# Scaling the experts' tokens by 1/rms once, at the turn, and modulating a whole gather on ScalarE

## The chip, the cores and the metric

The kernel runs on one core of one Trainium2 chip. The metric is the device time of one execution in microseconds; three runs of the kernel before gave 1472.24 to 1476.46, with a median of 1474.25. The core's engines each work through their own queue in order: TensorE (PE in the profile) multiplies and turns matrices, VectorE (DVE) and ScalarE (ACT) work on elements, SyncE (SP) starts the transfers from memory. They wait for each other by semaphores.

## The reference, cut to what matters

A two-layer backbone over 256 tokens of width 1024. The change concerns only the second half of its second layer, a mixture of eight experts, of which each token goes to its best two. What goes into it is the stream `h`, brought to unit rms, scaled and shifted per channel:

```python
def rmsnorm(x, g):
    xf = x.astype(jnp.float32)
    y = xf * lax.rsqrt(jnp.mean(xf * xf, axis=-1, keepdims=True) + EPS)
    return (y * g.astype(jnp.float32)).astype(x.dtype)

def modulate(x, g, shift, scale):
    return rmsnorm(x, g) * (1 + scale) + shift

def swiglu(h, wg, wu, wd):
    return (jax.nn.silu(h @ wg) * (h @ wu)) @ wd

def moe_swiglu(h, router_w, wg, wu, wd):
    logits = (h @ router_w).astype(jnp.float32)
    top_v, top_i = lax.top_k(logits, TOP_K)
    gates = jax.nn.softmax(top_v, axis=-1)
    ...
    out = jnp.zeros_like(h)
    for e in range(N_EXPERTS):
        out = out + dense_gate[..., e:e + 1] * swiglu(h, wg[e], wu[e], wd[e])
    return out
```

Each expert has `wg` and `wu` of 1024 x 3584 and `wd` of 3584 x 1024, in fp32. The result is added to the stream, which is the output.

## The kernel before

**Products.** fp32 values go through PE as pairs of a rounded value ("hi") and the rest ("lo"). A heavy expert (more than 64 tokens) takes three products per pair (lines 142 to 144, in `mm3`), a light one two (lines 1078 and 1079); which arm runs is decided on PE by a branch on the expert's count.

**The turn of the tokens.** The stream lies transposed in `hT` (channels on partitions). Its sums of squares give `rstd`, two columns of 1/rms for the two times 128 tokens (`mo_v` in the trace). Sixteen PE transposes turn the tokens into four banks `mo{t}{b}` of PSUM, and ACT copies each bank (128 x 512) into `h`, in which tokens lie on partitions (L1001). `h` isn't scaled by `rstd`. Beside it run the router: `lg`, the ranks, `posm` (each token's place in each expert) and `gates()` with an exponent on ACT (L1031), for which ACT loads a table of functions.

**An expert's gather.** `Expert.positions()` makes one-hot matrices from `posm` on DVE: `oh`, `ohd` (each place twice, for light experts) and `ohs`, which is `oh` with `rstd` in the place of the ones (L1098). `gather(b)` picks the expert's tokens, for the channels' lower (b = 0) and upper half (b = 1): eight PE products `h` x `ohs` into one bank (`m_pg`, L1109), then the modulation `t32 = pg * a + b` in four pieces of 128 x 128 (`m_t`): for b = 0 on DVE (L1118), for b = 1 on ACT (L1116). `split_pairs` makes the hi (ACT, L217) and lo (DVE, L218) of `xg`, the input of the gate and up products. Both halves use one bank in turn, since that pool has one buffer; expert 0 takes two banks of another pool.

**The weights.** Each expert is worked in seven chunks of 512 columns; a chunk has three groups of two tiles of 1 MB: gate, up, and the down tiles of the chunk before. The class `Weights` brings in the 336 tiles: `load` starts a transfer on SP's queue into a raw buffer (`mw`), `split` casts it to hi on ACT (`mh`, L948) and takes hi from it to lo on DVE (`ml`, L949). `group()` runs the products of a group, splits the tiles of the groups ahead between them and then runs closures put off until there (`late`). Positions and both halves of the gather for the next expert are put off in this way, too: they stand behind the fifth chunk (`ci == NCH - 3`) of each expert, positions there, the halves behind one group each (`after(0)`, `after(1)`).

**The end of an expert.** The down products end in two banks; `gated` and `scatter` multiply them back to the tokens' places and add them on DVE: `acc = ps * gate + was` (L1184). For expert 0 `was` is `h` itself (the stream), so that the stream is added; for the others it is `acc`.

**What sets the order.** The Tile scheduler puts the instructions of each engine in an order from dependences and its own costs. By hand only a little is fixed: `behind["A"]` holds the first casts of weights behind the last copy of `h` (`copied`) on ACT, `behind["V"]` the first subtractions behind expert 0's `xg` (`ex.made`) on DVE.

Of the kernel before, what the change touches and what calls it, by code (L numbers as in the profile page):

```python
# [13 lines left out]
AF = mybir.ActivationFunctionType  # L14
ALU = mybir.AluOpType
# [3 lines left out]
P = 128  # L19
D = 1024  # L20
KT = D // P
S = 256
NT = S // P
# [51 lines left out]
def hybrid_kernel(  # L75
# [6 lines left out]
    V, A, T = nc.vector, nc.scalar, nc.tensor  # L82
# [13 lines left out]
    def slot(i, name, dt=F32):  # L96
        return ap_.tile([P, 2056 if i == 7 else 2048], dt, tag=f"s{i}", name=name)

    def x2k(name, dt=F32):
        return xp.tile([P, 512], dt, tag="x2k", name=name)  # L100

    def bank(name, pool=None):
        pool = pool or psa
        return pool.tile([P, 512], F32, tag="bank", name=name)
# [36 lines left out]
    def mm3(o, lh, ll, rh, rl, start, stop):  # L141
        T.matmul(o, lh, rh, start=start, stop=False)  # L142
        T.matmul(o, lh, rl, start=False, stop=False)  # L143
        T.matmul(o, ll, rh, start=False, stop=stop)  # L144
# [213 lines left out]
    def flush():  # L358
        while waiting:
            waiting.pop(0)()  # L360
# [76 lines left out]
    def mod_tiles(s_hi, s_lo, name):  # L437
        return tuple(slot(i, f"{name}_{x}", F32R)[:, :KT * S].rearrange("p (k t) -> p k t", k=KT) for i, x in ((s_hi, "hi"), (s_lo, "lo")))
# [10 lines left out]
    class Rows:  # L449
# [6 lines left out]
        def one(self, i, k, wh, wl):  # L456
            hi, lo, t, _ = self.specs[i]
            mm3(self.pss[i], hi[:, k, t * P:(t + 1) * P], lo[:, k, t * P:(t + 1) * P], wh, wl, start=(k == 0), stop=(k == KT - 1))
# [200 lines left out]
    y = mod_tiles(2, 3, "y")  # L659
# [294 lines left out]
    m_m = Mod(1, 3, 0, R_FFN + KT, "a_m")  # L954
# [30 lines left out]
    gate = kp.tile([P, NT, NE], F32, name="gate")  # L985
# [6 lines left out]
        next_ada()  # L992
    del behind["T"]
    rstd = st.rstd()
    h = slot(2, "h")[:, :NT * D].rearrange("p (t d) -> p t d", t=NT)
    for t in range(NT):
        for b in range(2):
            pt = bank(f"mo{t}{b}", psc)
            for i in range(4):
                T.transpose(pt[:, i * P:(i + 1) * P], hT[:, 4 * b + i, t * P:(t + 1) * P], ident)  # L1000
            copied = A.copy(h[:, t, b * 512:(b + 1) * 512], pt)  # L1001
    behind["A"] = copied.ins
    lg = kp.tile([P, NT, NE], F32, name="lg")
    for t in range(NT):
# [39 lines left out]
        return nc.values_load(flag[0:1, 0:1], min_val=0, max_val=1)  # L1044

    at = slot(3, "moe_aT", F32R)
    acc = slot(4, "moe_acc")[:, :NT * D].rearrange("p (t d) -> p t d", t=NT)
    iota = cst[:, C_IOTA:C_IOTA + P]

    def pick(w, e, *at):  # L1050
# [9 lines left out]
    def split_pairs(v, src):  # L1060
        return split_to(v[:, :, :, 0], v[:, :, :, 1], src.rearrange("p (k s) -> p k s", s=P))
# [24 lines left out]
    class Expert:  # L1086
# [5 lines left out]

        def positions(self):
            oh2 = x2k(self.n + "_oh")
            self.oh, self.ohs = oh2[:, :S], oh2[:, S:]
            self.ohd = x2k(self.n + "_ohd")[:, :S]
            for t in range(NT):
                V.tensor_scalar(self.ohs[:, t * P:(t + 1) * P], iota, one(self.pos, t, self.e), rstd[t], op0=ALU.is_equal, op1=ALU.mult)  # L1098
            for t in range(NT):
                for o, at_ in ((self.oh, iota), (self.ohd, twice)):  # L1100
                    V.tensor_scalar(o[:, t * P:(t + 1) * P], at_, one(self.pos, t, self.e), None, op0=ALU.is_equal)

        def gather(self, b, pool=None):
            n = self.n
            pg = bank(f"{n}_pg{b}", pool or psd)
            for i in range(4):
                k = 4 * b + i
                for t in range(NT):
                    T.matmul(pg[:, i * P:(i + 1) * P], h[:, t, k * P:(k + 1) * P], self.ohs[:, t * P:(t + 1) * P],  # L1109
                             start=(t == 0), stop=(t == NT - 1))  # L1110
            t32 = x2k(f"{n}_t{b}")
            for i in range(4):
                k = 4 * b + i
                o = slice(i * P, (i + 1) * P)
                if b:
                    A.activation(t32[:, o], pg[:, o], AF.Identity, bias=m_m.b(k), scale=m_m.a[:, k:k + 1])  # L1116
                else:
                    V.tensor_scalar(t32[:, o], pg[:, o], m_m.a[:, k:k + 1], m_m.b(k), op0=ALU.mult, op1=ALU.add)  # L1118
            self.made = split_pairs(self.xg[:, 4 * b:4 * b + 4], t32)

        def places(self, light):
# [19 lines left out]
        def turn(self, pts, gu, light):  # L1141
            for pt, src in zip(pts, gu):
                for i in range(4):
                    o = pt[:, i * P:(i + 1) * P]
                    if light:
                        T.matmul(o, src[:, i * P:(i + 1) * P], fold, start=True, stop=True)
                    else:
                        T.transpose(o, src[:, i * P:(i + 1) * P], ident)
# [26 lines left out]
            split_to(*y, src)  # L1175
            return y

        def scatter(self, t, i, y, first=False, pool=None):

            ps = bank(f"{self.n}_sc{t}{i}", pool or psd)  # L1180
            for o in range(2):
                T.matmul(ps, self.ohT[:, t * P:(t + 1) * P], y[o], start=(o == 0), stop=(o == 1))
            av, was = (a[:, t, i * 512:(i + 1) * 512] for a in (acc, h if first else acc))
            V.scalar_tensor_tensor(av, ps, one(gate, t, self.e), was, op0=ALU.mult, op1=ALU.add)  # L1184

    def store(t, i):
        nc.sync.dma_start(out[0, t * P:(t + 1) * P, i * 512:(i + 1) * 512], acc[:, t, i * 512:(i + 1) * 512])
# [20 lines left out]
    def after(n, f):  # L1208
        todo_after.setdefault(step + n, []).append(f)
# [19 lines left out]
    def turned(x, ci, gu):  # L1229
        pts = [bank(f"{x.n}_{ci}_t{m}", psb) for m in range(2)]  # L1230
        return pts, (lambda arm: x.turn(pts, gu, arm)), (lambda: x.act(ci, pts))
# [3 lines left out]
    for e in range(NE):  # L1235
        light = lights[e]
        for ci in range(NCH):
            gu = []
            _, turn, acted = turned(ex, ci - 1, prev[2]) if ci else nothing
            if ci:  # L1240
                behind.clear()
            o = bank(f"{ex.n}_{ci}_0")
            places = ci == 0
            if places:
                ex.po = bank(ex.n + "_ohp", psb)

            def gates_up(parts, arm, o=o):
                turn(arm)
                if places:
                    ex.places(arm)  # L1250
                ex.up(o, parts, arm)

            def gates_then(o=o, ex=ex, ci=ci, gu=gu, acted=acted, places=places):
                if places:
                    ex.placed()
                acted()
                gu.append(ex.copied(o, f"{ex.n}_{ci}_g"))

            group(light, gates_up, gates_then)
            u = bank(f"{ex.n}_{ci}_1")  # L1260
            group(light, lambda parts, arm: ex.up(u, parts, arm), lambda u=u, x=ex, ci=ci, gu=gu: gu.append(x.copied(u, f"{x.n}_{ci}_u")))
            if (e, ci) == (0, 1):
                over = gates()
                flush()
            if prev is not None:
                px, pi, _ = prev
                if pi == 0:
                    px.y = [bank(f"{px.n}_y{i}", psc) for i in range(2)]
                if ci == NCH - 1:
                    _, turn, acted = turned(ex, ci, gu)  # L1270
                else:
                    turn, acted = nothing[1:]

                def downs(parts, arm):
                    px.down(pi, parts, arm)
                    turn(arm)

                def downs_then(acted=acted, px=px, pi=pi):
                    acted()
                    if pi == NCH - 1:  # L1280
                        ys = [px.gated(i) for i in range(2)]
                        for i in range(2):
                            for t in range(NT):
                                after(1 + 2 * i + t, lambda x=px, t=t, i=i: x.scatter(t, i, ys[i], first=x.e == 0))

                group(lights[px.e], downs, downs_then)
            if ci == NCH - 3 and e + 1 < NE:
                nxt = Expert(e + 1, posm, (e + 1) % 2, f"m{e + 1}")
                nxt.positions()
                for b in range(2):  # L1290
                    after(b, lambda b=b, x=nxt: x.gather(b))
            prev = (ex, ci, gu)
        last = ex
        if e + 1 < NE:
            ex = nxt
            lights[e + 1] = nc.values_load(few[0:1, e + 1:e + 2], engines=(mybir.EngineType.PE,), min_val=0, max_val=1)
    for i in range(2):
        group(lights[-1], lambda parts, arm: last.down_half(i, parts, arm))
        y = last.gated(i)
# [5 lines left out]
    with tc.If(over > 0):  # L1305
        pos2 = sp.tile([P, NT, NE], F32, tag="pos2", name="pos2")
        V.tensor_scalar(pos2, posm, -float(P), None, op0=ALU.add)
        with tc.For_i(0, NE) as ev:
# [9 lines left out]
            for ci in range(NCH):  # L1318
                gu = []
                for m in range(2):  # L1320
                    o = bank(f"v_{ci}_{m}")
# [6 lines left out]
            for i in range(2):  # L1328
                y = ex.gated(i)
# [57 lines left out]
```

## Time and profile before

| | |
|---|---|
| median of three runs | 1474.25 us (1472.24 to 1476.46) |
| profiled execution | 1478.5 us, span in the trace 1476.7 us |
| TensorE, busy | 1390.9 us (94%) |
| TensorE, weight loads | 1151.7 us (78%) |
| VectorE, busy | 1226.8 us (83%) |
| ScalarE, busy | 974.0 us (66%) |
| the chain that ended last, by engine | PE 59%, DVE 20%, issue 9%, ACT 8%, DMA 5% |
| read from memory | 470.64 MB |
| the 336 subtractions of L949 | 757.1 us busy, 2286 ns each |
| the 336 casts of L948 | 631.2 us busy, 1910 ns each |

Busy time is the time in which an engine had an instruction running, as a share of the span; overlapping instructions of one engine are not counted twice. The chain is followed back from the last instruction to what released it each time; "issue" is time in which the engine waited for nothing that the profile shows. The experts run from about 507 us to the end, one behind the other, in stretches of 90 to 131 us, so that shares over the span mix two layers and eight stretches; stretches are looked at apart below.

### The profile page before, as it was taken

The page shows a single profiled execution, that of the slowest core. Times are in us where ns is not written, and L with a number is a line of the kernel's source. Part 1 is how long each engine was busy: PE and PEld are TensorE (multiplying, and loading weights), DVE is VectorE, ACT ScalarE, POOL GpSimd, SP SyncE. Part 2 cuts the span into 40 slices and gives each one's busy share as a digit, 9 for nine tenths or more (in the row PEclk, how much of TensorE's full clock was granted, in tenths as well). Part 3 has the DMA queues.
Part 4 walks back from the last instruction along what each step waited for, and adds up shares of the span by engine and source line. Part 5 has one row for each costly group of instructions (what it writes and reads, how often), then busy time and mean ns, then how long its engine had stood idle before and what let it go on. Part 6 is the DMA issues. An engine that isn't in the chain of part 4 may idle for free.

```text
span 1476.7 us, 19854 instructions
## 1 busy us (share of the span) xinstructions
PE 1390.9 (94%) x7746; PEld 1151.7 (78%) x7746; DVE 1226.8 (83%) x1256; ACT 974.0 (66%) x891; POOL 1.9 (0%) x7
## 2 busy tenths in 40 slices
PE   6999999999999999999989989999999999899897
PEld 4667789999979888877767767777888888677675
DVE  4687588776666698899999998998888879899897
ACT  3444354433354576788887887886777768788785
POOL 0000000000000000000000000000000000000000
PEclk9999999999999999999999999999999999999999
DMA  9554488776654698899998998998978988899894
GB/s 367 226 219 166 155 335 323 286 274 251 245 224 176 240 402 330 326 340 395 403 398 343 408 398 334 416 385 338 365 294 331 365 343 349 331 421 386 336 413 189
DMA packets 66784, 473.53 MB, mean 321 GB/s; under 512 B 7376, under 2 KB 7760, under 8 KB 9696
## 3 DMA queue, kind: packets, MB, share of 16 engines
q1 hardware_dynamic: 66464, 471.16, 82.0%
q8 instruction: 93, 1.52, 0.4%
q0 software_dynamic: 192, 0.56, 0.2%
q14 instruction: 35, 0.29, 0.1%
HBM read 470.64 MB, written 1.05 MB: 319 GB/s over the span
## 4 chain that ended last, share of the span: by engine, by line
PE 59%; DVE 20%; issue 9%; ACT 8%; DMA 5%; DVEq 0%; SPq 0%; ACTq 0%
DVE ml L949 13%; ACT mh L948 5%; PE m L142 5%; PE m L144 5%; PE m L143 5%; PE fg_ps L164 4%; PE fd L164 4%; PE fu_ps L164 4%; PE m_y L144 2%; PE m_y L142 2%; PE m_y L143 2%; PE so_ps L164 2%; PE ada L259 2%; PE su_ps L164 2%; DMA mw<-in_moe_w_gate_dram 1%
## 5 line engine op out<-in xcount | busy, mean ns | idle before, releaser
L949 DVE TENSOR_TENSOR ml<-mw,mh 128x2048 fp32r<-128x2048 f32 x336 | 757.1, 2286 | 47.9 <-ACT mh L948 44.9
L948 ACT CAST mh<-mw 128x2048 fp32r<-128x2048 f32 x336 | 631.2, 1910 | 12.4 <-PE so_ps L164 4.1
L1079 PE MATMUL m<-ml,m_xg 128*128 128x512 f32 x560 | 223.3, 399 | 5.7 <-DVE ml L949 5.7
L1078 PE MATMUL m<-mh,m_xg 128*128 128x512 f32 x560 | 224.1, 400 | 0.0
L1078 PE MATMUL m_y<-mh,moe_aT 128*128 128x512 f32 x280 | 118.2, 422 | 25.3 <-DVE moe_aT L218 21.4
L142 PE MATMUL m<-mh,m_xg 128*128 128x512 f32 x336 | 134.5, 401 | 0.6 <-ACT m_xg L217 0.6
L1079 PE MATMUL m_y<-ml,moe_aT 128*128 128x512 f32 x280 | 121.3, 433 | 13.8 <-DVE ml L949 11.9
L1079 PEld LDWEIGHTS m<-ml,m_xg 128*128 128x128 f32 x560 | 105.2, 188 | 37.0 <-DVE ml L949 14.6
L144 PE MATMUL m<-mh,m_xg 128*128 128x512 f32 x336 | 132.9, 396 | 0.0
L143 PE MATMUL m<-ml,m_xg 128*128 128x512 f32 x336 | 132.7, 395 | 0.0
L1078 PEld LDWEIGHTS m<-mh,m_xg 128*128 128x128 f32 x560 | 105.3, 188 | 22.6
L1079 PEld LDWEIGHTS m_y<-ml,moe_aT 128*128 128x128 f32 x280 | 56.4, 201 | 45.3 <-DVE ml L949 34.3
L1078 PEld LDWEIGHTS m_y<-mh,moe_aT 128*128 128x128 f32 x280 | 56.7, 203 | 41.3 <-ACT mh L948 19.3
L217 ACT CAST moe_aT<-m_sg 128x512 fp32r<-128x512 f32 x56 | 37.4, 669 | 72.5 <-DVE m_sg L1153 72.5
L142 PEld LDWEIGHTS m<-mh,m_xg 128*128 128x128 f32 x336 | 65.6, 195 | 13.3 <-ACT m_xg L217 1.5
L144 PEld LDWEIGHTS m<-mh,m_xg 128*128 128x128 f32 x336 | 65.5, 195 | 12.5
L143 PEld LDWEIGHTS m<-ml,m_xg 128*128 128x128 f32 x336 | 65.7, 196 | 11.9
L1152 ACT ACTIVATE m_sg<-m_t 128x512 f32<-128x512 f32 x56 | 33.6, 599 | 53.5 <-PE m L142 26.7
L144 PE MATMUL m_y<-mh,moe_aT 128*128 128x512 f32 x168 | 66.4, 396 | 0.7 <-DVE moe_aT L218 0.7
L143 PE MATMUL m_y<-ml,moe_aT 128*128 128x512 f32 x168 | 66.4, 395 | 0.0
L142 PE MATMUL m_y<-mh,moe_aT 128*128 128x512 f32 x168 | 66.2, 396 | 0.0
L164 PE MATMUL fd<-a,fd_hi 128*128 128x256 f32 x352 | 63.0, 281 | 0.0
(410 smaller groups left out, 2663.8 us busy)
## 6 DMA issues: line engine op xcount, KB each, us to landing
mw<-in_moe_w_gate_dram SPq DMA_DIRECT2D x112, 1024.0 KB, 7.1
mw<-in_moe_w_up_dram SPq DMA_DIRECT2D x112, 1024.0 KB, 7.1
mw<-in_moe_w_down_dram SPq DMA_DIRECT2D x110, 1024.0 KB, 6.8
ada<-in_ada_w_dram SPq DMA_DIRECT2D x40, 1024.0 KB, 4.9
fg_w<-in_ffn_w_gate_dram SPq DMA_DIRECT2D x11, 1024.0 KB, 5.2
fu_w<-in_ffn_w_up_dram SPq DMA_DIRECT2D x11, 1024.0 KB, 5.4
fd<-in_ffn_w_down_dram SPq DMA_DIRECT2D x11, 1024.0 KB, 5.0
adap<-in_ada_pairs_dram SPq DMA_DIRECT2D x8, 1024.0 KB, 9.6
```

The source lines that it names most:

```text
L142: T.matmul(o, lh, rh, start=start, stop=False)
L143: T.matmul(o, lh, rl, start=False, stop=False)
L144: T.matmul(o, ll, rh, start=False, stop=stop)
L164: self.newest = m = T.matmul(o, lhsT, rhs, start=self.first is None, stop=stop, skip_group_check=True)
L217: A.copy(hi, src)
L259: queued(T.matmul(pa[32 * j:32 * j + 32, :r.shape[2]], stat[:, 4 * half + j, :], r[:, j, :], start=(first and half == 0), stop=(last and h ...
L948: queued(A.copy(hi, r), "A")
L949: queued(V.tensor_tensor(lo, r, hi.bitcast(F32), op=ALU.subtract), "V")
L1078: T.matmul(o, x, wh, start=start, stop=False)
L1079: T.matmul(o, x, wl, start=False, stop=stop)
L1152: A.activation(sg, pts[0], AF.Silu)
```

## The change

At the turn, each bank is now read by ACT twice: copied into `acc` (unscaled, the stream that the experts are added to), and copied times `rstd` into `h`. For this `acc` is made here, together with `h`; the two lie in slots of their own. `ohs` goes, and `oh` takes its place in the gather's products, since `h` already has the factor; `ohd` moves into the buffer that `ohs` had. The modulation is done by ACT in both halves of a gather. `scatter` always adds to `acc`.

```diff
@@ the turn of the tokens
-    h = slot(2, "h")[:, :NT * D].rearrange("p (t d) -> p t d", t=NT)
+    h, acc = (slot(i, n)[:, :NT * D].rearrange("p (t d) -> p t d", t=NT) for i, n in ((2, "h"), (4, "moe_acc")))
...
-            copied = A.copy(h[:, t, b * 512:(b + 1) * 512], pt)
+            at_ = slice(b * 512, (b + 1) * 512)
+            A.copy(acc[:, t, at_], pt)
+            copied = A.activation(h[:, t, at_], pt, AF.Copy, scale=rstd[t])
@@ Expert.positions
-            self.oh, self.ohs = oh2[:, :S], oh2[:, S:]
-            self.ohd = x2k(self.n + "_ohd")[:, :S]
-            for t in range(NT):
-                V.tensor_scalar(self.ohs[:, t * P:(t + 1) * P], iota, one(self.pos, t, self.e), rstd[t], op0=ALU.is_equal, op1=ALU.mult)
+            self.oh, self.ohd = oh2[:, :S], oh2[:, S:]
@@ Expert.gather
-                    T.matmul(pg[:, i * P:(i + 1) * P], h[:, t, k * P:(k + 1) * P], self.ohs[:, t * P:(t + 1) * P],
+                    T.matmul(pg[:, i * P:(i + 1) * P], h[:, t, k * P:(k + 1) * P], self.oh[:, t * P:(t + 1) * P],
...
-                if b:
-                    A.activation(t32[:, o], pg[:, o], AF.Identity, bias=m_m.b(k), scale=m_m.a[:, k:k + 1])
-                else:
-                    V.tensor_scalar(t32[:, o], pg[:, o], m_m.a[:, k:k + 1], m_m.b(k), op0=ALU.mult, op1=ALU.add)
+                A.activation(t32[:, o], pg[:, o], AF.Identity, bias=m_m.b(k), scale=m_m.a[:, k:k + 1])
@@ Expert.scatter
-            av, was = (a[:, t, i * 512:(i + 1) * 512] for a in (acc, h if first else acc))
-            V.scalar_tensor_tensor(av, ps, one(gate, t, self.e), was, op0=ALU.mult, op1=ALU.add)
+            av = acc[:, t, i * 512:(i + 1) * 512]
+            V.scalar_tensor_tensor(av, ps, one(gate, t, self.e), av, op0=ALU.mult, op1=ALU.add)
```

The scheduler's order changes with it. On ACT at the turn of the tokens, before; `mo_48..` are the banks with the turned tokens, `ex` the exponents of the gates, `ada_11_rw` a row of the modulation of this layer, `mh` the first casts of weights:

```order
L1001 COPY h<-mo_4855 128x512
L1031 ACT_TABLE_LOAD
L1031 ACTIVATE ex_5127<-lg,mx_5124 128x8
L264 COPY ada_11_rw<-ada_10_4796 128x512
L1001 COPY h<-mo_4861 128x512
L948 CAST mh_4946<-mw_4932 128x2048
```

The same place in the changed kernel, with `mo_v` the 1/rms:

```order
L1002 COPY moe_acc<-mo_4851 128x512
L1003 ACTIVATE h<-mo_4844,mo_v 128x512
L1003 ACTIVATE h<-mo_4851,mo_v 128x512
L1033 ACT_TABLE_LOAD
L1033 ACTIVATE ex_5128<-lg,mx_5125 128x8
L264 COPY ada_11_rw<-ada_10_4796 128x512
L1002 COPY moe_acc<-mo_4858 128x512
L1003 ACTIVATE h<-mo_4858,mo_v 128x512
L1002 COPY moe_acc<-mo_4865 128x512
L1003 ACTIVATE h<-mo_4865,mo_v 128x512
L948 CAST mh_4947<-mw_4933 128x2048
```

Two scaled copies now stand ahead of the table load, and four passes instead of one between the row of the modulation and the first cast.

On ACT in expert 1, where its sixth chunk meets the gather for expert 2, before (`m_5_g` and `m_5_u` are that chunk's gate and up results, copied; branches are the end of a light expert's arm):

```order
L1138 COPY m_5_g<-m_5_0_6867 128x512
L948 CAST mh_6938<-mw_6745 128x2048
L948 CAST mh_6967<-mw_6758 128x2048
L1194 UNCONDITIONAL_BRANCH
L1138 COPY m_5_u<-m_5_1_6937 128x512
L217 CAST m_xg<-m_t_6960 128x512
L948 CAST mh_7014<-mw_6805 128x2048
L1116 ACTIVATE m_t_7031<-m_pg_7022,modT,a_m 128x128 x4
L948 CAST mh_7038<-mw_6813 128x2048
L1194 UNCONDITIONAL_BRANCH
L217 CAST m_xg<-m_t_7031 128x512
```

The same place in the changed kernel:

```order
L1133 COPY m_5_g<-m_5_0_6862 128x512
L1113 ACTIVATE m_t_6955<-m_pg_6946,modT,a_m 128x128 x3
L948 CAST mh_6933<-mw_6743 128x2048
L1113 ACTIVATE m_t_6955<-m_pg_6946,modT,a_m 128x128
L217 CAST m_xg<-m_t_6955 128x512
L948 CAST mh_6962<-mw_6756 128x2048
L1189 UNCONDITIONAL_BRANCH
L1133 COPY m_5_u<-m_5_1_6932 128x512
L1113 ACTIVATE m_t_7026<-m_pg_7017,modT,a_m 128x128
L948 CAST mh_7009<-mw_6803 128x2048
L1113 ACTIVATE m_t_7026<-m_pg_7017,modT,a_m 128x128 x3
L217 CAST m_xg<-m_t_7026 128x512
```

Three of the first half's `m_t` stand ahead of the first cast and one behind it; of the second half's, one stands ahead of the third cast and three behind it. The first half's `m_xg` has moved ahead of the second cast.

On PE, the second half of that gather stands in one piece before, behind the down products:

```order
L144 MATMUL m_y_6220<-mh_6938,moe_aT 128x512
L1194 UNCONDITIONAL_BRANCH
L1109 MATMUL m_pg_7022<-m_oh,h 128x128 x8
L1194 COMPARE_AND_BRANCH
L1146 MATMUL m_5_t_7085<-fold,m_5_g 128x128 x4
```

In the changed kernel, from the end of the up products to the end of the down products:

```order
L144 MATMUL m_5_1_6932<-mh_6863,m_xg 128x512
L1189 UNCONDITIONAL_BRANCH
L1107 MATMUL m_pg_7017<-m_oh,h 128x128 x5
L1189 COMPARE_AND_BRANCH
...
L144 MATMUL m_y_6218<-mh_6933,moe_aT 128x512
L1189 UNCONDITIONAL_BRANCH
L1107 MATMUL m_pg_7017<-m_oh,h 128x128 x3
L1189 COMPARE_AND_BRANCH
L1141 MATMUL m_5_t_7080<-fold,m_5_g 128x128 x4
```

Five of the eight products have moved ahead of the down products, three stay behind them.

## Rows read from the trace of the kernel before

**Rows 1.** Windows: stretch, length, PE, PEld, DVE, ACT, POOL busy, PEclk, DMA share, GB/s.

```profile
510.00:600.00 90.00, 90.00 (x418) 75.89 (x417) 76.66 (x52) 66.57 (x51) 0.00 (x0) 1.00 0.91 353
627.00:742.00 115.00, 105.69 (x516) 83.47 (x515) 110.90 (x78) 96.41 (x81) 0.00 (x0) 1.00 0.97 380
742.00:858.00 116.00, 104.51 (x492) 81.54 (x491) 110.22 (x77) 95.11 (x80) 0.00 (x0) 0.97 0.96 382
974.00:1103.00 129.00, 127.45 (x592) 107.09 (x590) 110.93 (x77) 94.81 (x79) 0.00 (x0) 1.00 0.90 341
```

**Rows 2.** Groups, 732 to 848: count | busy us, mean ns | idle before.

```profile
L1118 DVE TENSOR_SCALAR m_t<-m_pg,a_m,modT 128x128 f32<-128x128 f32 x4 | 1.4, 404 | 0.0
L1098 DVE TENSOR_SCALAR m_oh<-cst,posm,mo_v 128x128 f32<-128x128 f32 x2 | 0.7, 342 | 0.0
```

**Rows 3.** Timeline of DVE in expert 1: start, us, instruction, count [idle before <-releaser].

```profile
705.97 0.34 DVE L1098 TENSOR_SCALAR m_oh<-cst,posm,mo_v 128x128 f32<-128x128 f32 x1
706.23 0.28 DVE L1101 TENSOR_SCALAR m_oh<-cst,posm 128x128 f32<-128x128 f32 x1
...
717.02 0.40 DVE L1118 TENSOR_SCALAR m_t<-m_pg,a_m,modT 128x128 f32<-128x128 f32 x1
717.35 2.28 DVE L949 TENSOR_TENSOR ml<-mw,mh 128x2048 fp32r<-128x2048 f32 x1
...
726.73 2.29 DVE L949 TENSOR_TENSOR ml<-mw,mh 128x2048 fp32r<-128x2048 f32 x1 [1.13 <-ACT mh L948]
...
732.94 6.69 DVE L949 TENSOR_TENSOR ml<-mw,mh 128x2048 fp32r<-128x2048 f32 x3
```

**Rows 4.** Timeline of ACT in the same stretch, around the gather.

```profile
714.34 0.67 ACT L217 CAST moe_aT<-m_sg 128x512 fp32r<-128x512 f32 x1 [1.15 <-DVE m_sg L1153]
...
715.38 3.72 ACT L948 CAST mh<-mw 128x2048 fp32r<-128x2048 f32 x2
...
720.62 0.67 ACT L217 CAST m_xg<-m_t 128x512 fp32r<-128x512 f32 x1 [1.05 <-DVE m_t L1118]
721.18 1.89 ACT L948 CAST mh<-mw 128x2048 fp32r<-128x2048 f32 x1
723.40 1.50 ACT L1116 ACTIVATE m_t<-m_pg,modT,a_m 128x128 f32<-128x128 f32 x4 [0.33 <-PE m_pg L1109]
724.78 1.91 ACT L948 CAST mh<-mw 128x2048 fp32r<-128x2048 f32 x1
...
733.09 3.72 ACT L948 CAST mh<-mw 128x2048 fp32r<-128x2048 f32 x2
```

**Rows 5.** Timeline of PE in the same stretch: first down product, then the gather's products.

```profile
717.27 0.45 PE L1078 MATMUL m_y<-mh,moe_aT 128*128 128x512 f32 x1
...
721.41 1.95 PE L1109 MATMUL m_pg<-m_oh,h 128*128 128x128 f32 x16
```

**Rows 6.** Timelines of ACT, DVE and PE at the turn, to the first expert product.

```profile
494.49 1.07 ACT L1001 COPY h<-mo 128x512 f32<-128x512 f32 x2 [0.16 <-PE mo L1000]
495.58 1.28 ACT L1031 ACT_TABLE_LOAD   x1
...
499.87 0.58 ACT L1001 COPY h<-mo 128x512 f32<-128x512 f32 x1
500.35 3.70 ACT L948 CAST mh<-mw 128x2048 fp32r<-128x2048 f32 x2
...
505.94 0.65 ACT L217 CAST m_xg<-m_t 128x512 fp32r<-128x512 f32 x1
...
497.01 0.28 DVE L210 SCALAR_TENSOR_TENSOR mo_v<-mo_a,mo_y 128x1 f32<-128x1 f32 x2
...
501.20 3.73 PE L1109 MATMUL m_pg<-m_oh,h 128*128 128x128 f32 x32
...
506.65 0.51 PE L142 MATMUL m<-mh,m_xg 128*128 128x512 f32 x1 [0.64 <-ACT m_xg L217]
```

**Rows 7.** Timelines of PE and DVE, and a window, at the start of expert 2.

```profile
769.64 0.76 PE L1078 MATMUL m_y<-mh,moe_aT 128*128 128x512 f32 x1 [4.59 <-DVE moe_aT L218]
...
776.78 0.75 DVE L1184 SCALAR_TENSOR_TENSOR moe_acc<-m_sc,gate,moe_acc 128x512 f32<-128x512 f32 x1 [4.43 <-PE m_sc L1182]
...
769.00:777.00 8.00, 7.10 (x18) 5.30 (x18) 3.57 (x4) 6.05 (x5) 0.00 (x0) 0.59 0.92 353
```

More of the change, by code (lines that the diff above doesn't have):

```diff
@@ L1046, in hybrid_kernel @@
     at = slot(3, "moe_aT", F32R)
-    acc = slot(4, "moe_acc")[:, :NT * D].rearrange("p (t d) -> p t d", t=NT)
     iota = cst[:, C_IOTA:C_IOTA + P]
@@ L1176, in gated, with scatter @@
             return y
-        def scatter(self, t, i, y, first=False, pool=None):
+        def scatter(self, t, i, y, pool=None):
             ps = bank(f"{self.n}_sc{t}{i}", pool or psd)
@@ L1283, in downs_then @@
                             for t in range(NT):
-                                after(1 + 2 * i + t, lambda x=px, t=t, i=i: x.scatter(t, i, ys[i], first=x.e == 0))
+                                after(1 + 2 * i + t, lambda x=px, t=t, i=i: x.scatter(t, i, ys[i]))
                 group(lights[px.e], downs, downs_then)
```

## Prediction

> **What bounds the kernel now.** I read the page first, then the stretches by window, then single queues. Before 480 us nothing that the diff touches runs. From 510 on the kernel turns through eight experts with two regimes. In the first one TensorE (PE) is busy all the time (510 to 600: 90.00 of 90 us); 974 to 1103, and 1103 to 1234 like it, are also PE's (127.45 of 129). In 742 to 858 it is VectorE (DVE) that has 110.22 of 116 us and PE 104.51; 627 to 742 is like it [rows 1], and so are 858 to 974 and 1234 to 1349. So there are three experts at PE's pace (0, 4, 5: all three products per pair) and five at DVE's (1, 2, 3, 6, 7: two products). A gather of the next expert stands in experts 0 to 6; four of these seven (1, 2, 3, 6) are at DVE's pace. Time taken from DVE can count only there.
>
> Within such an expert a tile of weights goes DMA, ACT cast (mh), DVE subtraction (ml), PE. ACT has 95.11 of 116 us [rows 1], so it looks free; but it is one queue in order, and the timeline around a gather shows how little room its casts have. DVE waits 1.13 us for a cast at 726.73 [rows 3], because ACT had first waited 1.05 us for DVE's modulation (720.62), then 0.33 for PE, then run four m_t [rows 4]. That is the place to look at: the change takes work from DVE and puts it in front of those casts.
>
> **The change, part by part.**
>
> *DVE's saving in a gather.* Two m_oh with rstd and four m_t leave: 0.7 and 1.4 us of busy time [rows 2]. An instruction begins a little before the end of the one ahead, so what counts is the distance of starts: 705.97 to 706.23 for m_oh (0.26), 717.02 to 717.35 for m_t (0.33) [rows 3]. 2 x 0.26 + 4 x 0.33 = 1.8 us per gather; 4 x 1.8 = 7.3 us in the experts at DVE's pace. This is the most that can be won there. In experts 0, 4 and 5 PE's work covers it.
>
> *ACT's addition in a gather.* Four more m_t: the four of now take 723.40 to 724.78, 0.345 each [rows 4], so 1.4 us. It is not spread: three of the four stand ahead of the cast that starts at 715.38 and the fourth, with m_xg, behind it; of the second half one stands ahead of the cast of 721.18, three ahead of that of 724.78.
>
> *Whether the 1.8 us arrive.* I walk expert 1's gather with the new order and the durations of [rows 3, 4]. DVE reaches the chunk's splits 0.5 us earlier (m_oh). The scheduler then puts m_sg one split earlier, which makes ACT's m_sg, that waits for PE's turn, go ahead of a cast; that cast starts later by about as much, so DVE's gain of 0.5 is used up. ACT's moe_aT no longer waits until 714.34 but runs at 711.7, m_5_g at 714.0, when PE has its input, then three m_t: the cast of 715.38 starts at 715.5, its DVE partner at 717.5 instead of 717.35, with DVE idle 0.95 before it. The last m_t of the first half and m_xg end at 718.3; nothing waits for DVE's modulation now, so the 1.05 us of idle at 720.62 go. The cast of 721.18 starts at 720.85. Then three m_t wait for the last three products of the gather. These stand on PE behind the same down products as now and come at 723.4, when the sixteen m_pg of now end (721.41 + 1.95) [rows 5]: PE does five of the eight products before the down products, but needs the same work by then. So m_t runs at 723.5 to 724.5, m_xg to 725.2, and the cast of 724.78 starts at 725.1, 0.3 later; DVE idles 1.1 us before its partner, about as at 726.73 today. The next casts are 0.7 and 1.6 us early, but ACT's moe_aT waits for DVE's m_sg, which now stands behind one more split, at 731.4, and behind moe_aT and m_g stands the cast of 733.09, which by this starts at 733.2. Its DVE partner is the second of the three at 732.94: 735.1 then and now. From there the order is that of before until the next gather. So DVE's 1.8 us turn into 2 us of waits for ACT, and the gain per expert is 0 (between -1.8, if ACT keeps its lead, and +1.4, if all that ACT gets is late). I take -0.1 each, -0.4 in four.
>
> *The wait that is new on PE.* Both halves of a gather share one bank; the second half's five products, now ahead of the down products, wait for ACT's fourth m_t (717.8), and queued behind them are the down products. PE comes there at 717.3 [rows 5] and the second tile of the down products is not split before 719.6 (717.35 + 2.28), so 0.5 us of wait cost nothing in experts at DVE's pace. In those at PE's pace 24 up products stand on PE between the two halves of the gather, 6.2 us (16 down products take 717.27 to 721.41, 0.26 each [rows 5]); the four m_t and a cast among them take 1.4 + 1.9: covered, unless that cast is late by more than 2 us.
>
> *The turn of the tokens, once.* The critical chain from 495 to 506 is not PE at its peak but ACT's queue: ada_rw, the last copy of h at 499.87, three casts from 500.35 on, m_xg at 505.94, first product at 506.65 [rows 6]. In the new order ACT has 4 copies into acc and 4 scaled ones into h instead of 4 copies. Two scaled ones need rstd, ready between 497.01 and 497.29 [rows 6], and stand ahead of the table load that now runs at 495.58 while ACT would wait anyway. No scaled one is in the trace; I take 0.58, the whole duration of a copy, for its distance, and 0.48 for a copy (two take 1.07 us [rows 6]). So 2 x 0.58: 498.4; the load of 1.28: 499.7; the exponent, and ada_rw to 500.2. Then copy, scaled, copy, scaled, 2 x (0.48 + 0.58): casts begin at 502.3, 1.9 us later than 500.35. Ahead of m_xg then stand two casts and five m_t (2 x 1.8 + 5 x 0.345 = 5.3 us) instead of three casts: m_xg at 507.6, first product at 508.3, +1.65. The second half of xg (511.7 and 512.3 by the same walk) lets PE wait some 0.3 more, since three m_t and a cast now stand before it. PE's gather itself starts later too (503.1 for 501.2 [rows 6]; it waits for two posm and gate steps behind ada_rw), but ends before ACT is at its m_t. Sum +2.0 us. Expert 0 is at PE's pace behind it, and then DVE's queue starts from where PE's stands, so it is carried to the end. Bounds: 0.6 if the scaled copies hide in the present wait for DVE and the load is earlier than I think, 3.6 if four more passes (4 x 0.58) and the load (1.28) all lie on the path.
>
> The load's price is read as 1.28 us: the copy ahead of it ends at 495.56 and the load begins at 495.58 [rows 6]. The Trainium skill (ScalarE: Activation LUTs, What ACT_TABLE_LOAD costs) adds about 1.38 us of drain to every switch of the set, which would make the turn +3.4 us and the forecast 1477.6; no row here shows that drain.
>
> *The rest.* One scratch buffer less per expert: allocations come looser, no wait of the trace names one; 0. acc in the first scatter instead of h: same form, 0. Load order on SP is the same.
>
> **Sum.** Profiled execution 1478.5 us (span 1476.7 and 1.8 around it): +2.0 - 0.4 = 1480.1. The median of the runs is 4.25 us lower (1474.25), so 1475.9, say 1476.
>
> **Rivals.**
> (1) *Forecast*: gather's gain lost to ACT's queue, turn +2: 1476 (1473.5 to 1479).
> (2) *DVE's gain arrives.* If the casts stay ahead of DVE, 7.3 us go and 2.0 come: 1469. For it: DVE is busy 95% of these experts, and two idle times on ACT (1.05, 1.15 [rows 4]) go. Against: DVE already waits for a cast right there [rows 3].
> (3) *ACT becomes the bound, slower.* If the last three gather products come later than 723.4, or the cast of 733.09 is late for any reason, every microsecond goes on to DVE, since DVE has no store of finished casts there. The added m_t in full, 1.4 x 4 = 5.6, and 2.0: 1482. It decides from the point where ACT's cast starts after 733.1. The Trainium skill (ScalarE: Activation LUTs, Rules for kernel authors) gives multiplies and adds to VectorE rather than ScalarE, which speaks for this one.
> (4) *The clock.* In expert 2, and in 3, 6 and 7 in the same way, PE pauses 4.59 us for moe_aT, then its granted clock falls to its lower level (mean 0.59 in 769 to 777) and DVE waits 4.43 us for a scatter [rows 7]; expert 1 has no such fall (1.00 in 627 to 742 [rows 1]). A fall is worth at most that wait of 4.43, so one more or one less gives 1480 or 1472. DVE's order is unchanged there, so I expect the same four.
>
> **How the numbers follow.** Chances: (1) 0.62, (2) 0.17, (3) 0.14, (4) 0.07. About 0.3% (4.4 us) is what a measurement of this kernel can tell from no change. (1) and (4) lie within it; (2) lies at -0.36% and a partial gain is within, so faster 0.15; (3) at +0.5%, slower 0.15; same 0.70. Range: 1468.5 to 1482, from (2) to (3), leaving out a tenth on each side.
>
> **What would show it.** First expert product at about 508.3 instead of 506.65, and all of expert 0 late by 2. In experts 1, 2, 3, 6 DVE's busy time 2 us lower with as much more waiting for mh, the period still 116. Wrong if the period of these experts falls by a microsecond or more (then 2) or rises (then 3), or if the table load stands elsewhere.

## The result: slower by 1.1%, and where the time went

| | before | changed |
|---|---|---|
| median of the runs | 1474.93 us (1472.24 to 1476.46) | 1491.79 us (1490.57 to 1491.98) |
| ratio to the kernel before, 95% interval | | 1.0112 (1.0100 to 1.0124) |
| profiled execution, span | 1478.5, 1476.7 us | 1491.63, 1489.9 us |

The forecast was 1476 with a range from 1468.5 to 1482: the time lies beyond it. The page of the changed kernel, its busy times and its chain of work; L1113 is now the line of m_t, L1107 that of m_pg:

```profile
PE 1391.2 (93%) x7746; PEld 1148.0 (77%) x7746; DVE 1214.5 (82%) x1208; ACT 987.0 (66%) x927; POOL 1.9 (0%) x7
...
PE 58%; DVE 19%; ACT 10%; issue 9%; DMA 3%; DVEq 0%; SPq 0%; ACTq 0%
```

DVE has 12.3 us less to do (1226.8 before) and ACT 13.0 more (974.0), as the change says; PE has the same. ACT, which took the work over, is busy for 66% of the span, as before. What grew is waiting. The groups that show it, first of the kernel before, then of the changed one (count | busy us, mean ns | idle time before them, and what ended it):

```profile
L949 DVE TENSOR_TENSOR ml<-mw,mh 128x2048 fp32r<-128x2048 f32 x336 | 757.1, 2286 | 47.9 <-ACT mh L948 44.9
...
L1116 ACT ACTIVATE m_t<-m_pg,modT,a_m 128x128 f32<-128x128 f32 x32 | 12.1, 455 | 11.0 <-PE m_pg L1109 11.0
```

```profile
L949 DVE TENSOR_TENSOR ml<-mw,mh 128x2048 fp32r<-128x2048 f32 x336 | 757.4, 2285 | 65.9 <-ACT mh L948 62.8
...
L1113 ACT ACTIVATE m_t<-m_pg,modT,a_m 128x128 f32<-128x128 f32 x64 | 25.7, 467 | 24.7 <-PE m_pg L1107 24.7
```

The subtractions wait 17.9 us more for ACT's casts, and ACT's m_t wait 13.7 us more for PE's gather. Most of both happens at one place. ACT's queue there, in expert 1 (rows of before: [rows 4]; columns: start, us, instruction, count, idle time before and what ended it):

```profile
717.97 0.48 ACT L1113 ACTIVATE m_t<-m_pg,modT,a_m 128x128 f32<-128x128 f32 x1
718.48 0.68 ACT L217 CAST m_xg<-m_t 128x512 fp32r<-128x512 f32 x1
719.05 1.90 ACT L948 CAST mh<-mw 128x2048 fp32r<-128x2048 f32 x1
720.84 0.58 ACT L1133 COPY m_u<-m 128x512 f32<-128x512 f32 x1
724.32 0.46 ACT L1113 ACTIVATE m_t<-m_pg,modT,a_m 128x128 f32<-128x128 f32 x1 [2.90 <-PE m_pg L1107]
724.67 1.89 ACT L948 CAST mh<-mw 128x2048 fp32r<-128x2048 f32 x1
726.47 1.16 ACT L1113 ACTIVATE m_t<-m_pg,modT,a_m 128x128 f32<-128x128 f32 x3
```

PE's gather of the second half, and DVE's subtraction behind that cast, in the changed kernel ([rows 5] and [rows 3] before):

```profile
718.50 1.38 PE L1107 MATMUL m_pg<-m_oh,h 128*128 128x128 f32 x10 [0.31 <-ACT m_t L1113]
...
723.45 0.83 PE L1107 MATMUL m_pg<-m_oh,h 128*128 128x128 f32 x6
...
726.60 2.29 DVE L949 TENSOR_TENSOR ml<-mw,mh 128x2048 fp32r<-128x2048 f32 x1 [3.33 <-ACT mh L948]
```

One m_t of the second half stands in ACT's queue ahead of a weight cast. The products that it reads were done by 719.9 (718.50 + 1.38; the trace counts two instructions for a product), but it starts at 724.32, 0.04 us after the last product of the bank (723.45 + 0.83). It waits for the whole bank, and three products of that bank stand behind the down products on PE. The other traces agree: in none of the thirteen, in none of the gathers for experts 1 to 7, does an m_t start before the last product of its bank has ended (the nearest comes 0.04 us behind it). Whether the program or the chip asks for that isn't shown here. The cast behind it starts at 724.67 instead of 721.18, and DVE, which has no finished cast in store, waits 3.33 us.

What that costs is read between two subtractions on either side of the gather, eighteen tiles apart, the same two in both kernels. Before:

```profile
691.31 4.49 DVE L949 TENSOR_TENSOR ml<-mw,mh 128x2048 fp32r<-128x2048 f32 x2
...
739.54 4.49 DVE L949 TENSOR_TENSOR ml<-mw,mh 128x2048 fp32r<-128x2048 f32 x2
```

Changed:

```profile
691.98 4.49 DVE L949 TENSOR_TENSOR ml<-mw,mh 128x2048 fp32r<-128x2048 f32 x2
...
742.65 4.49 DVE L949 TENSOR_TENSOR ml<-mw,mh 128x2048 fp32r<-128x2048 f32 x2
```

48.23 us and 50.67. This **gather stretch** is the same to 0.04 us in experts 1, 2, 3 and 6 of a kernel, so one of them measures an order of instructions there better than any median does. The spans' difference of 13.1 us is, place by place: -2.6 before the turn (the last write of the stream ends at 493.51 and 490.94; chance, see below), +1.8 at the turn, +0.4 in expert 0, +1.0 where expert 1 begins, 4 x 2.43 = +9.7 in experts 1, 2, 3 and 6, +4.0 in experts 4 and 5, -3.3 at the scatters of experts 3, 6 and 7, and +2.0 in the last 18 us.

The +1.0 is a second place of the same kind. On ACT, where expert 1 begins, two casts stood ahead of an m_sg that waits for PE, and now only one does; the other comes behind the wait. Before:

```profile
623.28 3.71 ACT L948 CAST mh<-mw 128x2048 fp32r<-128x2048 f32 x2
628.80 0.60 ACT L1152 ACTIVATE m_sg<-m_t 128x512 f32<-128x512 f32 x1 [1.81 <-PE m_t L1148]
```

Changed:

```profile
622.92 1.91 ACT L948 CAST mh<-mw 128x2048 fp32r<-128x2048 f32 x1
628.44 0.60 ACT L1147 ACTIVATE m_sg<-m_t 128x512 f32<-128x512 f32 x1 [3.61 <-PE m_t L1143]
628.93 1.90 ACT L948 CAST mh<-mw 128x2048 fp32r<-128x2048 f32 x1
```

PE then waits 0.46 us for a cast at 633.72. No run alters this order alone, so that it makes the +1.0 is read from the rows and not shown.

### The profile page after: what moved, and what is told of

It is laid out like the page before. It is cut to its first block, busy times and chain, and to the rows that moved or that the text cites. A ratio compares the mean times of both kernels' runs of the same rounds, so it can differ in the third digit from the quotient of the medians.

```text
span 1489.9 us, 19842 instructions
## 1 busy us (share of the span) xinstructions
PE 1391.2 (93%) x7746; PEld 1148.0 (77%) x7746; DVE 1214.5 (82%) x1208; ACT 987.0 (66%) x927; POOL 1.9 (0%) x7
## 4 chain that ended last, share of the span: by engine, by line
PE 58%; DVE 19%; ACT 10%; issue 9%; DMA 3%; DVEq 0%; SPq 0%; ACTq 0%
DVE ml L949 13%; ACT mh L948 7%; PE m L143 5%; PE m L144 5%; PE m L142 5%; PE fg_ps L164 4%; PE fd L164 4%; PE fu_ps L164 4%; PE m_y L144 3%; PE m_y L142 2%; PE m_y L143 2%; PE so_ps L164 2%; PE su_ps L164 2%; PE m_pg L1107 2%; PE m_y L1079 2%
## 5 line engine op out<-in xcount | busy, mean ns | idle before, releaser
L144 PE MATMUL m_y<-mh,moe_aT 128*128 128x512 f32 x168 | 66.4, 396 | 0.7 <-DVE moe_aT L218 0.7
L142 PE MATMUL m_y<-mh,moe_aT 128*128 128x512 f32 x168 | 66.4, 397 | 0.0
```

## Experiments

Theory W: the wait of that one m_t for its bank, with the cast queued behind it. Rivals: A, the four m_t that ACT has more per gather (1.4 us) are the cost by themselves; P, PE's five products ahead of the down products hold them up. Ratios are to the kernel before, run beside each (its medians were 1474.3 to 1476.0 us), with 95% intervals; the gather stretch was 48.24 us before and 50.67 in the changed kernel.

**ACT's order altered (e1_act_order).** `W.cast` is the newest weight cast:

```diff
-                A.activation(t32[:, o], pg[:, o], AF.Identity, bias=m_m.b(k), scale=m_m.a[:, k:k + 1])
+                m = A.activation(t32[:, o], pg[:, o], AF.Identity, bias=m_m.b(k), scale=m_m.a[:, k:k + 1])
+                if b and pool is None:
+                    tc.add_manual_dep(m.ins, W.cast.name, ..., reason="the order of the queue")
```

> The changed kernel with one order fixed: ACT's four m_t of a gather's second half stand behind the weight cast that is emitted before them (the third cast of the gather), as they did in the kernel before. Theory W (wait): in the changed kernel the first of them stood ahead of that cast and waited 2.90 us for the last product of the bank, and cast and subtraction behind it came 3.3 us late; with the order fixed the loss of 3.3 per gather falls to 0.5 or less, about 2.5 us in each of the six gathers of experts 1 to 6: 1491.6 - 15 = 1476.5, 1474 to 1480. Theory A (ACT's four added m_t, 1.4 us per gather, are the cost by themselves): the added work stays, 1475 + 7 x 1.4 = 1485 or more. Theory P (five of PE's products of the second half stand ahead of the down products and hold them): PE's order stays, so 1491.

1476.89 us, ratio 1.0023 (1.0011 to 1.0034); gather stretch 48.49. PE's order is the changed kernel's. The scheduler moved more by itself: behind the gather, the second half's m_xg stands one cast later on ACT, and m_sg one cast earlier on ACT and one subtraction earlier on DVE. So e1 alone doesn't single out the lone m_t; e2 does.

**Only PE's order altered (e2_pe_order).** The first product of each pair of the group behind the gather (in `mm3` likewise) is ordered behind the last of the gather's eight m_pg; the order of computing instructions on ACT and DVE is the changed kernel's, with the lone m_t still ahead of the cast.

```diff
-                    T.matmul(pg[:, i * P:(i + 1) * P], h[:, t, k * P:(k + 1) * P], self.oh[:, t * P:(t + 1) * P],
+                    m = T.matmul(pg[:, i * P:(i + 1) * P], h[:, t, k * P:(k + 1) * P], self.oh[:, t * P:(t + 1) * P],
...
+            if b and pool is None:
+                behind["M"] = m.ins
...
-            T.matmul(o, x, wh, start=start, stop=False)
+            queued(T.matmul(o, x, wh, start=start, stop=False), "M")
```

> The changed kernel with PE's order fixed instead: all eight products of a gather's second half stand ahead of the down products (five did, three stood behind them); ACT and DVE have the changed kernel's order. Theory W: the bank is full some 3 us earlier, before ACT comes to the first m_t of the second half, so that its wait of 2.90 us goes though it still stands ahead of the cast: 1475 to 1480, as in e1_act_order. Theory A: 1485 or more. Theory P: PE's down products wait for ACT even more (three products more in front of them): 1491 or slower.

1474.57 us, ratio 0.9989 (0.9977 to 1.0002); gather stretch 47.70. ACT in expert 2's gather:

```profile
839.60 0.47 ACT L1115 ACTIVATE m_t<-m_pg,modT,a_m 128x128 f32<-128x128 f32 x1
839.95 1.91 ACT L948 CAST mh<-mw 128x2048 fp32r<-128x2048 f32 x1
```

PE's gather in front of it:

```profile
836.78 2.05 PE L1107 MATMUL m_pg<-m_oh,h 128*128 128x128 f32 x16 [0.33 <-ACT m_t L1115]
```

The bank is full at 838.83, ACT comes at 839.60 and waits for nothing. The time is 0.4 us below the range expected. Two edits, made on different engines, each end the wait ahead of that cast, and each takes away all or most of the loss. As causes of the loss A and P fall: ACT does the same work in both, and in e2 even more products stand ahead of the down products. A small loss of P's kind remains, as e4 will show.

**The two halves of the change apart (e3_turn_only, e4_mod_only).** e3 has the scaled turn, acc and the gather with `oh`, and the old modulation; e4 has only this:

```diff
-                if b:
-                    A.activation(t32[:, o], pg[:, o], AF.Identity, bias=m_m.b(k), scale=m_m.a[:, k:k + 1])
-                else:
-                    V.tensor_scalar(t32[:, o], pg[:, o], m_m.a[:, k:k + 1], m_m.b(k), op0=ALU.mult, op1=ALU.add)
+                A.activation(t32[:, o], pg[:, o], AF.Identity, bias=m_m.b(k), scale=m_m.a[:, k:k + 1])
```

> Half of the change: the tokens are multiplied by 1/rms once at the turn and copied into acc, and the matrix with rstd goes; the modulation stays as before (first half on DVE, second on ACT). Theories W and A: no m_t stands ahead of the third cast, nothing is added to ACT in a gather, DVE loses two instructions (0.5 us per gather) and the first expert product is 0.7 us earlier as in the changed kernel: 1474.9 - 6 x 0.5 - 0.7 = 1471, 1469.5 to 1475. The step of the prediction that priced the turn at +2.0 would give 1476 to 1477. If the loss of 16.7 us sits in this half: above 1485.

> The other half of the change: all of a gather's modulation on ACT; the tokens are turned and the matrix with rstd is made as in the kernel before. In this build the order has the third cast ahead of all four m_t of the second half, and the m_t of the first half two and two around the first cast. Theory W: the wait has no cast behind it that is early enough to matter; DVE's four m_t go (1.3 us per gather): 1470 to 1478. Theory A: 1474.9 + 7 x 1.4 = 1485. If all-ACT modulation is the whole loss whatever the order: 1490.

e3: 1477.47 us, 1.0022 (1.0010 to 1.0034), gather stretch 48.51. e4: 1479.70 us, 1.0031 (1.0019 to 1.0043), gather stretch 49.39. Each half alone costs a little, neither has the loss: the bad place in ACT's queue comes only with the order that both together got. My expectation for e3 was a miss, and the older one, that of the prediction (1476 to 1477), came within half a microsecond: the turn took 1.9 us more, as it said, and the gathers 0.27 each, which it had near nothing. DVE's 0.5 us per gather don't arrive. Its wait for the cast behind the four m_t, which wait for PE, only grows, 1.48 in e3 where the kernel before had 1.15:

```profile
837.18 1.51 ACT L1114 ACTIVATE m_t<-m_pg,modT,a_m 128x128 f32<-128x128 f32 x4 [0.47 <-PE m_pg L1107]
...
840.51 2.29 DVE L949 TENSOR_TENSOR ml<-mw,mh 128x2048 fp32r<-128x2048 f32 x1 [1.48 <-ACT mh L948]
```

So this cast too is set by when PE fills the bank, before as after. In e4, which came out 1.7 us above the range that theory W gave it, the four m_t of the second half stand behind the third cast, and the loss per gather is 1.15. That is near ACT's added 1.4, but PE's row in expert 1 tells another cause:

```profile
716.68 1.16 PE L1109 MATMUL m_pg<-m_oh,h 128*128 128x128 f32 x8 [1.30 <-ACT m_t L1115]
```

Four products of the second half now stand ahead of the down products, both halves share one bank, and PE waits 1.30 us until ACT has read the first half out of it. The down products and the rest of the gather come later by that. Counted from the start of the gather stretch, the bank is full at 32.06 us before, 32.30 in e1, 32.32 in e3 and 33.21 in e4, so 0.24, 0.26 and 1.15 later; the stretches are 0.25, 0.27 and 1.15 longer. In these four kernels a cast stands right behind the four m_t, and the time at which the bank is full sets the pace. The loss of e4 is theory P in the small, and not A.

**The second half of the gather put off (e5_spread, before_spread).** Of the changed kernel and of the kernel before:

```diff
-                    after(b, lambda b=b, x=nxt: x.gather(b))
+                    after(3 * b, lambda b=b, x=nxt: x.gather(b))
```

> The changed kernel with the second half of each gather put off by three groups instead of one (so the two halves stand in two chunks). Orders of ACT and PE are left to the scheduler. By the wait theory the m_t of the second half now stand behind the seventh chunk's casts' start and find their bank full: no wait of 2.90. If ACT's queue in the one chunk that holds both halves is what is left (in e2_pe_order DVE still waits 0.73, 0.35 and 0.66 us for casts there), two of the three waits go: 47.7 us for the three stretches around a gather become about 46.5, 6 x 1.2 less at most and the four at DVE's pace for certain: 1474.6 - 5 = 1469.5, 1467 to 1473. If the casts can't use the room (the ring of casts or the transfers hold them): 1474 to 1477. If the scratch buffers that are held longer make DVE or ACT wait: above 1478.

> The kernel before with only the same move of the second half by three groups. It says whether the spreading needs the change at all. DVE keeps its six instructions (1.8 us per gather), its wait of 1.15 for a cast behind the four m_t goes: 4 x 1.15 less, 1475.5 - 4.6 = 1471, 1469 to 1474. If that wait comes back elsewhere: 1474 to 1477.

e5: 1472.70 us, 0.9984 (0.9973 to 0.9995), gather stretch 47.38. before_spread: 1472.38 us, 0.9994 (0.9984 to 1.0003), gather stretch 48.08. The first is the one version here whose interval lies below the kernel before, by a sixth of a per cent; it is 1.3% below the changed kernel. Both times lie in the ranges expected, but not by the way expected: the stretch was to fall to about 46.5 in e5 and by 1.15 in before_spread, and fell to 47.38 and by 0.16. Nor do they show that the change pays: the kernel before with the same move takes the same time. The change then saves 0.7 us per gather (47.38 against 48.08) and loses 2.9 at the turn, 1.1 of it with the lower clock (below). ACT's m_t never wait in e5, and the subtractions wait less than in any other version with the change (in before_spread 40.4 us in all):

```profile
L949 DVE TENSOR_TENSOR ml<-mw,mh 128x2048 fp32r<-128x2048 f32 x336 | 758.3, 2285 | 42.0 <-ACT mh L948 39.0
...
L1113 ACT ACTIVATE m_t<-m_pg,modT,a_m 128x128 f32<-128x128 f32 x64 | 25.8, 471 | 0.0
```

**The turn (pe_dveturn, spread_dveturn, spread_lateacc).** From the end of the stream's last write to the first expert product it takes 13.14 us before, 12.90 in e4, which has the old turn, and 14.98, 14.97 and 15.03 in the changed kernel, e1 and e3. In e2 and e5 it takes 16.09 and 16.08; there PE's 32 products for the modulation vector ran partly at the lower of the clock's two levels (mean granted clock 0.67 in 494.2 to 499.4 of e5) and took 5.34 us, in the changed kernel 3.64. Two ways were tried to get the 1.8 us back. DVE makes the scaled copies, on e2's order and on e5's:

```diff
-            A.copy(acc[:, t, at_], pt)
-            copied = A.activation(h[:, t, at_], pt, AF.Copy, scale=rstd[t])
+            copied = A.copy(acc[:, t, at_], pt)
+            V.tensor_scalar(h[:, t, at_], pt, rstd[t], None, op0=ALU.mult)
```

> e2_pe_order with the turn altered: DVE makes the scaled copies into h (4 of 128 x 512), ACT only the plain ones into acc. In the changed kernel and in e1, e2 and e3 the way from the last write of the stream to the first expert product takes 14.97 to 16.09 us against 13.14 before and 12.90 in e4_mod_only, which has the old turn. If ACT's four added passes there are the 1.8 us: 13.1 or a little less, and 1474.6 - 1.8 = 1472.8, 1471 to 1474.5. If what is late is PE's gather, which waits for all of h whoever writes it: 14.5 or more and 1474 to 1476.

> Both: the second half three groups later, and the scaled copies on DVE, without any fixed order. If the two gains add: e5_spread less 1.8 us, 1466 to 1471. If only one of the two holds, as that one alone.

pe_dveturn: 1477.10 us, 1.0012 (0.9998 to 1.0026), turn 17.98. spread_dveturn: 1472.32 us, 0.9989 (0.9978 to 1.0000), turn 16.34. The shorter turn is a miss in both, and the time of spread_dveturn is that of e5 alone: two of the copies now stand in DVE's queue ahead of the router's first step (they start at 496.86 in pe_dveturn, the router at 498.18), which PE's gather needs as well, and the other two wait 1.51 us for ACT's copies. PE's gather starts 12.0 us after the last write there (505.30 against 493.30), 9.8 in the changed kernel (500.77, 490.94). Part of the 12.0 is the clock: the 32 products took 5.34 us in pe_dveturn too (mean granted clock 0.68). In spread_dveturn they took 3.64, and the gather starts after 10.4. And the copies into acc put behind the first group, from four banks at once:

```diff
-            pt = bank(f"mo{t}{b}", psc)
+            pt = bank(f"mo{t}{b}", (psc, psd, psa, psa)[2 * t + b])
...
-            A.copy(acc[:, t, at_], pt)
+            turned_in.append((acc[:, t, at_], pt))
...
+            while turned_in:
+                A.copy(*turned_in.pop(0))
             u = bank(f"{ex.n}_{ci}_1")
```

> e5_spread with the plain copies into acc put behind the first group's products (the turned tokens stand in four banks at once, so that the copies can wait); ACT still makes the four scaled copies. DVE in place of ACT for those made the turn longer (16.34 and 17.98 us from the stream's last write to the first expert product, against 14.97 to 16.09), so writer and queue both count. If the four added passes ahead of the weight casts are the cost: 13.1 to 13.6 us for the turn and 1472.7 - 1.8 to 2.9 = 1470 to 1471. If what is late is the gather behind h, which now waits for 1/rms: 15 or more, and 1472 to 1474.

1475.42 us, 0.9998 (0.9985 to 1.0011), turn 16.90. A miss again, in time and turn: the scheduler now put one scaled copy behind two weight casts (502.56), and PE's second half of the gather waits 1.73 us for it. Whether a turn as short as the old one can be had with scaled tokens stays open; the orders tried took 1.8 to 4.8 us more, the longest with the lower clock in it.

**The same kernels again (after_again, before_again).**

> The changed kernel once more, unaltered, to part what belongs to it from what one profiled execution has by chance. Belonging to it by the wait theory: three stretches around a gather of 50.67 us in experts 1 to 3 and 6 and a wait of 2.90 for the bank; 14.98 us at the turn. By chance, if the clock's fall in the last 18 us is one: an end of 16.3 instead of 18.3 us after the last subtraction, and a start of the turn that lies up to 3 us elsewhere. Time 1490 to 1493.

> The kernel before once more, unaltered, for the same: 13.1 us at the turn and 48.2 us around a gather again, the end at 16.3 or 18.3 and the start of the turn up to 3 us elsewhere. Time 1472 to 1479.

1490.36 us, 1.0099 (1.0081 to 1.0117), and 1476.93. Turn 14.98 and 13.15, gather stretches 50.67 and 48.24: these belong to the order. The last write of the stream ended at 488.93 and 489.87 this time: that is chance, so -2.6 in the sum above is none of the change's. The end after the last subtraction took 17.94 us in the changed kernel and 16.69 in that before (18.32 and 16.32 the first time), so whether the longer end belongs to the order stays open.

## Why the prediction was wrong, point by point

*What bounds the kernel.* Right for the pace of the experts, and right that ACT's queue at the gather was the place to look at.

*Whether DVE's 1.8 us arrive.* The step that failed is one sentence of the walk: "The cast of 721.18 starts at 720.85." It let the lone m_t ahead of that cast run when ACT came to it, and made only the three behind wait for PE's last three products. Measured: 2.90 us of wait, and the cast at 724.67. Up to there the walk held: the first cast was said for 715.5 and came at 716.17, in a stretch that began 0.67 us later (691.98 against 691.31). The rows to know it by were there. In [rows 4] the first of the four m_t starts at 723.40, and PE's sixteen m_pg end at 723.36 [rows 5]; it too waited for the bank's last product, although its own two products are the first of the eight in the code. I read this as "m_t comes after m_pg" and not as a wait for all of the bank. Instead of -0.1 per gather the cost was +2.43. With the lone m_t behind its cast (e1) the walk's result holds, nearly: +0.25 (48.49 against 48.24), which is PE's new wait (below).

*Rival 3* had the place and the kind (ACT's casts late, every microsecond goes on to DVE), and the price wrong: it took ACT's added work, 1.4 us per gather, for what could be late. No run shows that price: e4's 1.15 is a wait of PE. What counted was the wait moved in front of the cast: 2.90 us on ACT, 3.33 on DVE, 2.43 of the stretch.

*Four of the seven gathers count.* Wrong. In experts 4 and 5 I let PE's work cover everything. There the down products are longer (three products per pair), so the lone m_t waits 6.19 us in expert 4; DVE waits 6.62 us for the cast, and PE then 0.74 and 0.48 for subtractions. By PE's products the two experts together take 3.7 us longer:

```profile
1091.28 0.46 ACT L1113 ACTIVATE m_t<-m_pg,modT,a_m 128x128 f32<-128x128 f32 x1 [6.19 <-PE m_pg L1107]
...
1093.57 2.29 DVE L949 TENSOR_TENSOR ml<-mw,mh 128x2048 fp32r<-128x2048 f32 x1 [6.62 <-ACT mh L948]
...
1095.91 0.51 PE L143 MATMUL m<-ml,m_xg 128*128 128x512 f32 x1 [0.74 <-DVE ml L949]
...
1099.46 0.51 PE L143 MATMUL m<-ml,m_xg 128*128 128x512 f32 x1 [0.48 <-DVE ml L949]
```

*The wait that is new on PE.* There, 0.31 us at 718.50 in the rows above, 0.5 said. That it costs nothing was wrong where a cast stands behind the bank: in e1 it goes with the 0.25 per gather, and in e4 a wait of 1.30 costs 1.15. In e2, with the same wait (0.33), all eight products stand ahead of the down products, and the stretch is shorter.

*The turn.* Right: +1.65 to the first product said, +1.84 measured (14.98 against 13.14), in the order that was said, and 0.3 behind it said, 0.37 measured by the end of expert 0 (m_sg at 628.44 and 628.80 above, each counted from its first product). ACT in the changed kernel, beside [rows 6]:

```profile
494.49 1.27 ACT L1003 ACTIVATE h<-mo,mo_v 128x512 f32<-128x512 f32 x2 [1.98 <-DVE mo_v L210]
495.77 1.28 ACT L1033 ACT_TABLE_LOAD   x1
497.07 0.30 ACT L1033 ACTIVATE ex<-lg,mx 128x8 f32<-128x8 f32 x1
...
498.22 0.70 ACT L1003 ACTIVATE h<-mo,mo_v 128x512 f32<-128x512 f32 x1
498.80 0.59 ACT L1002 COPY moe_acc<-mo 128x512 f32<-128x512 f32 x1
```

A scaled copy takes 0.70, and the next instruction starts 0.58 behind its start, as I took it. The first product itself came at 505.92, not at 508.3, since the turn began 2.6 us earlier: a sign given as a time on the clock was badly chosen, and a distance from the last write would have been the right one. The load stands between its neighbours with 0.01 and 0.02 us to spare. The Trainium skill (ScalarE: Activation LUTs, What ACT_TABLE_LOAD costs) adds about 1.38 us of drain to a switch; the trace shows no room for one here, so the row, not the page, gave the sum. The 1477.6 that the prediction gives for the page's rule leaves out its own -0.4 for the gathers; with it the sum is 1477.2.

*The clock.* The clock falls in experts 2, 3, 6 and 7 as before, but DVE's wait at the scatter shrinks in three of them (4.48 to 3.31 us in expert 3), which gives 3.3 us back. The last 18 us have a mean granted clock of 0.77 in the changed kernel and 0.85 before, and are 2.0 us longer. Neither was in the forecast. The end was long in e4 and pe_dveturn too (18.14, 18.21) and short in e1 and e2 (16.20, 16.67); what decides that I can't say.

## What to carry to other kernels

When a new order puts an instruction ahead of a cast that others live on, ask first what that instruction waits for, not how long it takes. To know this, look for the same kind of instruction in the trace of before and compare its start with the end of the *last* writer of its tile, not of its own part. The same holds for the tile's next writer: where two halves share a buffer, a write that moves ahead waits for the last reader (e4). Where such a wait turns up, it can be removed from either end: by the consumer's order (e1), by the producer's (e2), or by asking for the data later (e5).

## What was not expected

The gather stretch has a nearly fixed length for each order of instructions: in one kernel it agrees to 0.04 us between experts and between executions (what lies between the gathers of two light experts doesn't: 66.4 to 67.7 us in the changed kernel), while medians of whole runs move by 2 us and the start of the turn by 5 (488.36 to 493.51 in the kernels here). Differences of half a microsecond per gather can thus be read from one profile, where five rounds of timing leave 0.1% of doubt.
